# Modulation vectors by VectorE, GpSimd and ScalarE in four feed-forwards instead of by TensorE

## The chip, the cores and the metric

The kernel runs on one core of a Trainium2 chip. The metric is the device time of one execution in microseconds (us), the median of a few runs. A core has five engines with queues of their own, each in order: PE (TensorE, matmuls; PEld is its weight load), DVE (VectorE), ACT (ScalarE), POOL (GpSimd) and SP (SyncE, which issues the transfers here). They meet through semaphores. SBUF is the on-chip memory, PSUM the memory that PE writes.

## The reference, cut to what matters

Two networks of two layers run one after the other on 256 tokens of 1024 features, in float32. The second one is steered by modulation vectors, which come from two conditioning vectors and from nothing else:

```
for i in range(DEPTH):                      # DEPTH = 2
    m_lat = (silu(c) @ ada_w[i] + ada_b[i])      # [9 * 1024]
    m_ctx = (silu(c_ctx) @ ada_w[i] + ada_b[i])  # the same matrix
    sh1, sc1, gt1, sh2, sc2, gt2, sh3, sc3, gt3 = split(m_lat, 9)
    ...
    x = x + 0.5 * gt1 * swiglu(rmsnorm(x, g1) * (1 + sc1) + sh1, wi, wo)
    ...                                     # the context stream alike, with m_ctx
```

So for each layer a matrix of 1024 x 9216 (36 MB) is multiplied by two vectors. Around it stand eight feed-forwards (1024 to 2 x 2816 and back), a recurrent and attention mixer in each layer of the first block, a convolution module in layer 0 of the second block (for both streams, x and the context), and windowed attention in layer 1.

## The kernel before

Features lie on the partitions, tokens along the free dimension; X holds x in columns 0:256 and the context in 256:512. Every weight tile comes by SP into `wraw` (2 buffers of 1 MB, L275), ScalarE casts it to its high part `whi` (L281), VectorE subtracts that to get the low part `wlo` (L282), and PE makes each product from three matmuls (L294 to L296): high by high, high by low, low by high. Each part of eight 128x128 tiles is one 128x1024 pass; five buffers of each part let about two and a half chunks be ready ahead of PE.

A feed-forward has 22 inner tiles and 8 output tiles. In the first block (`ffn1st`, L408 to L430) an inner tile takes 48 matmuls of 256 columns, then VectorE multiplies the result out of PSUM by the norm (L420), ScalarE takes the silu (L422), VectorE multiplies (L424), and the product is split by ScalarE (L373) and VectorE (L374). An output tile takes 66 matmuls and an add into X (L370), and the following norm's input is made (L393, L370 into `big`) with its squares on GpSimd (`Sq`, L335, L341, L342). The second block's feed-forward (`Feed`) does the same for one stream (L889, L890, L373, L374) or both.

After each inner and output tile a `hook` is called. In the two feed-forwards of layer 0 of the first block it is `hook_ada`; in later ones `hook_bg` runs VectorE's share of the context's convolution in between.

The modulation vectors before: `ada(l, g)` is a generator, four of them with 18 steps each. A step loads 1 MB of `ada_w` into one of the large buffers (`big`, 13 of them), and issues four matmuls with 32 stationary columns, each in its own group of 32 columns of PE and each with 512 moving columns, all into one PSUM bank (L748; the profile has two records for each). After 18 steps ScalarE copies the bank out, 4 small matmuls with the selection `sel` bring the result to feature-major order (L756), and VectorE adds the bias (L759). `filler(n)` runs n steps. Layer 0's 36 steps come from `hook_ada`, layer 1's from the convolution of x (34 of them asked for there) and the feed-forward behind it. `prepare(l)` turns the scales into gains before they are used. The order in which instructions stand on each engine is set by a scheduler from the program's order and its own estimates; `after(newest[0])` holds a load behind the newest weight load on SP, and `after(newest[1])` a matmul behind the newest one.

## Time and profile before

| what | before |
|---|---|
| median of 3 runs | 3207.89 us (3207.72 to 3211.8) |
| the profiled execution: span from first to last instruction | 3207.8 us |
| PE busy | 3138.7 us, 98% |
| DVE busy | 1939.8 us, 60% |
| ACT busy | 1468.9 us, 46% |
| POOL busy | 341.5 us, 11% |
| moved by DMA | 536.02 MB, 167 GB/s on average |
| granted clock of TensorE, mean | 0.985 of full speed |

The page gives no time for the profiled execution but its span; it agrees with the median within 0.1 us. A row with `L282` is about line 282 of the kernel before; `out<-in` names what is written and read. "Busy" of PE is the union of modelled matmuls. In a row of the timeline the first number is the start in us from the span's start, the second the length, and x2 merges neighbours of one kind. A DVE or POOL instruction that stands waiting inside itself is counted as busy.

### The profile page before, as it was taken

What the parts mean: (1) busy time and instruction counts of PE and PEld (TensorE: products, weight loads), DVE (VectorE), ACT (ScalarE), POOL (GpSimd) and SP (SyncE); (2) the same over time, 40 slices, a digit from 0 to 9 for tenths busy, and PEclk for the clock granted to TensorE, in tenths of its full rate; (3) what the DMA queues carried; (4) which work ended last, traced back from release to release, by engine and by line L of the source; (5) the groups of instructions that cost most, each with busy time, mean ns of one, the idle gap of its engine ahead of it and who ended that gap; (6) DMA issues with size and microseconds to landing.
All of it is one profiled execution on the core that took longest, in us unless ns stands there. A gap on an engine that the chain in (4) does not pass through costs nothing.

```text
span 3207.8 us, 55462 instructions
## 1 busy us (share of the span) xinstructions
PE 3138.7 (98%) x23080; PEld 2916.9 (91%) x23080; DVE 1939.8 (60%) x3139; ACT 1468.9 (46%) x2421; POOL 341.5 (11%) x410
## 2 busy tenths in 40 slices
PE   9999999999999999999999999999999999999998
PEld 8899899999999999899999998878888888895898
DVE  6557666556558998668767557954333433356554
ACT  4446654445445446545555446643222322246443
POOL 1010102011010010001011025410002000110101
PEclk9999999999999999999999999989999999999999
DMA  7664346764454554345554554775222223230354
GB/s 284 266 231 164 127 163 238 272 221 167 172 183 171 177 188 166 129 160 188 178 175 159 173 169 168 279 285 188 92 87 97 98 88 110 77 112 34 132 177 139
DMA packets 84252, 536.02 MB, mean 167 GB/s; under 512 B 10016, under 2 KB 13088, under 8 KB 32416
## 3 DMA queue, kind: packets, MB, share of 16 engines
q1 hardware_dynamic: 84000, 532.48, 46.9%
q8 instruction: 180, 2.95, 0.4%
q14 instruction: 72, 0.59, 0.0%
HBM read 531.39 MB, written 1.05 MB: 166 GB/s over the span
## 4 chain that ended last, share of the span: by engine, by line
PE 92%; DVE 3%; ACT 1%; POOL 1%; issue 1%; DMA 1%; POOLq 0%; DVEq 0%; SPq 0%; ACTq 0%
PE psmm L294 28%; PE psmm L295 28%; PE psmm L296 28%; PE psad L748 2%; DVE wlo L282 1%; DVE big L370 1%; PE psad L1133 1%; PE psst L1125 1%; PE psst L350 1%; POOL tmp L342 1%; ACT whi L281 1%; DVE tmp L370 1%; PE psst L296 0%; PE psst L294 0%; PE psst L295 0%
## 5 line engine op out<-in xcount | busy, mean ns | idle before, releaser
L294 PE MATMUL psmm<-big,whi 128*128 128x256 f32 (+1 forms) x6546 | 1955.3, 300 | 14.8 <-ACT big L841 10.9
L295 PE MATMUL psmm<-big,whi 128*128 128x256 f32 (+1 forms) x6546 | 1955.6, 299 | 5.0 <-DVE big L370 5.0
L296 PE MATMUL psmm<-big,wlo 128*128 128x256 f32 (+1 forms) x6546 | 1952.6, 299 | 3.1 <-DVE wlo L282 3.1
L281 ACT CAST whi<-wraw 128x1024 fp32r<-128x1024 f32 (+2 forms) x940 | 904.6, 973 | 1320.4 <-PE psmm L295 941.8
L282 DVE TENSOR_TENSOR wlo<-wraw,whi 128x1024 fp32r<-128x1024 f32 (+2 forms) x940 | 1067.2, 1144 | 689.1 <-ACT whi L281 677.9
L294 PEld LDWEIGHTS psmm<-big,whi 128*128 128x128 f32 x6546 | 1260.6, 193 | 88.4 <-issue 19.8
L295 PEld LDWEIGHTS psmm<-big,whi 128*128 128x128 f32 x6546 | 1262.5, 193 | 46.7 <-issue 7.1
L296 PEld LDWEIGHTS psmm<-big,wlo 128*128 128x128 f32 x6546 | 1261.7, 193 | 44.4 <-issue 5.5
L335 POOL TENSOR_TENSOR tmp<-X 128x256 f32<-128x256 f32 x20 | 15.7, 792 | 1670.5 <-DVE X L370 1620.1
L370 DVE SCALAR_TENSOR_TENSOR big<-U,vec,big 128x256 f32<-128x256 f32 x392 | 188.9, 496 | 4.0 <-ACT big L977 0.5
L890 DVE TENSOR_TENSOR tmp<-tmp,psmm 128x256 f32<-128x256 f32 (+1 forms) x120 | 58.9, 491 | 122.8 <-PE psmm L296 118.7
L373 ACT CAST big<-tmp 128x256 fp32r<-128x256 f32 (+1 forms) x210 | 92.5, 441 | 82.8 <-DVE tmp L424 65.1
L420 DVE TENSOR_TENSOR tmp<-psmm,tmp 128x512 f32<-128x512 f32 x88 | 60.7, 690 | 106.3 <-PE psmm L296 105.5
L296 PE MATMUL psmm<-whi,big 128*128 128x256 f32 x416 | 118.3, 284 | 2.0 <-DVE big L370 2.0
L341 POOL TENSOR_TENSOR tmp<-X 128x256 f32<-128x256 f32 x100 | 83.9, 848 | 329.6 <-DVE X L370 272.5
L294 PE MATMUL psmm<-whi,big 128*128 128x256 f32 x416 | 118.8, 286 | 0.1
L295 PE MATMUL psmm<-wlo,big 128*128 128x256 f32 x416 | 118.1, 284 | 0.0
L374 DVE TENSOR_TENSOR big<-tmp,big 128x256 fp32r<-128x256 f32 (+1 forms) x210 | 97.7, 467 | 20.0 <-ACT big L373 19.4
L342 POOL TENSOR_TENSOR tmp<-tmp,tmp 128x256 f32<-128x256 f32 x100 | 102.6, 1030 | 5.3
L370 DVE SCALAR_TENSOR_TENSOR X<-psmm,mods,X 128x256 f32<-128x256 f32 x96 | 43.5, 480 | 74.7 <-PE psmm L296 72.9
L296 PEld LDWEIGHTS psmm<-whi,big 128*128 128x128 f32 x416 | 79.7, 192 | 2.4 <-DVE big L370 2.2
L295 PEld LDWEIGHTS psmm<-wlo,big 128*128 128x128 f32 x416 | 79.8, 192 | 0.1
(271 smaller groups left out, 2012.1 us busy)
## 6 DMA issues: line engine op xcount, KB each, us to landing
big<-ada SPq DMA_DIRECT2D x72, 1024.0 KB, 9.6
wraw<-fi_c SPq DMA_DIRECT2D x66, 1024.0 KB, 4.9
wraw<-fi_d SPq DMA_DIRECT2D x52, 1024.0 KB, 4.9
wraw<-fi_b SPq DMA_DIRECT2D x44, 1024.0 KB, 4.9
wraw<-fi_a SPq DMA_DIRECT2D x43, 1024.0 KB, 4.9
wraw<-fo_c SPq DMA_DIRECT2D x48, 704.0 KB, 4.0
wraw<-qkv SPq DMA_DIRECT2D x24, 1024.0 KB, 4.9
wraw<-pw SPq DMA_DIRECT2D x24, 1024.0 KB, 4.9
```

The lines of the kernel that those rows point to most:

```text
L281: A.copy(hi[:, :e], raw[:, o : o + e])
L282: V.tensor_sub(lo[:, :e], raw[:, o : o + e], hi[:, :e])
L294: T.matmul(o, wh, xh, start=start, stop=False)
L295: T.matmul(o, wh, xl, start=False, stop=False)
L296: newest[1] = T.matmul(o, wl, xh, start=False, stop=stop).ins
L341: G.tensor_tensor(out=q, in0=src, in1=src, op=ALU.mult)
L342: G.tensor_tensor(out=self.acc, in0=self.acc, in1=q, op=ALU.add)
L370: V.scalar_tensor_tensor(o, a, s, b, op0, op1)
L373: A.copy(hi, src)
L374: V.tensor_sub(lo, src, hi)
L420: V.tensor_tensor(out=v2(t), in0=v2(b), in1=pre.Rb, op=ALU.mult)
L748: T.matmul(p_[32 * q : 32 * q + 32, :], cs[:, 4 * h + q, 16 - 2 * b : 48 - 2 * b], raw[:, q * 512 : (q + 1) * 512], start=b == 0 and h == ...
```

## The change

The product with `ada_w` is turned: the matrix is laid out with output features on the partitions, so that each output is a sum along the free dimension of 1024 products. `Modulation.begin` loads silu's argument, the two conditioning vectors repeated on all partitions (`cs`, 1 MB), and takes the silu on ScalarE. `step` loads 256 outputs of `ada_w` (1 MB: two rows of 1024 for each partition) and works on what earlier steps loaded: VectorE multiplies by the context's vector and sums in the same instruction (its product, `junk`, is dropped), GpSimd multiplies by x's vector in place, and one step later ScalarE sums that by a copy with an accumulated output. `end` adds the bias of a whole layer. The steps of layer 0 stand in the same two feed-forwards as before, two of three inner tiles and the first five output tiles; those of layer 1 are moved forward, from the convolution of x and what follows it into the context's and x's first feed-forwards of the second block. The constants `sel`, `c`, `c_ctx` and the tile `cs` of the old form go; there are 14 large buffers for 13.

```diff
-NBIG = 13
+NBIG = 14
...
-        out[f"ada{l}"] = a["ada_w_2"][l].reshape(2, 4, P, 18, 512).transpose(3, 0, 2, 1, 4).reshape(18, 2, P, 2048)
+        out[f"ada{l}"] = a["ada_w_2"][l].T.reshape(36, 2, P, D).transpose(0, 2, 1, 3)
...
-    def ada(l, g):
-        p_ = ps("ad")
-        for b in range(9):
-            for h in range(2):
-                raw = bigt([P, 2048])
...
-                    nc.sync.dma_start(raw, I[f"ada{l}"][9 * g + b, h])
-                yield
-                with after(newest[1]):
-                    for q in range(4):
-                        T.matmul(p_[32 * q : 32 * q + 32, :], cs[:, 4 * h + q, 16 - 2 * b : 48 - 2 * b], raw[:, q * 512 : (q + 1) * 512], start=b == 0 and h == 0, stop=b == 8 and h == 1, tile_position=(0, 32 * q))
...
+    class Modulation:
+        def __init__(self):
+            self.todo = [(l, g) for l in range(2) for g in range(36)]
+            self.cs = self.here = self.made = None
+
+        def begin(self):
+            self.cs = bigt([P, 2, D])
+            with after(newest[0]):
+                nc.sync.dma_start(self.cs, I["cs"])
+            A.activation(self.cs, self.cs, AF.Silu)
+
+        def step(self, l, more=True):
+            if self.made:
+                raw, o = self.made
+                for i in range(2):
+                    A.activation(raw[:, i], raw[:, i], AF.Copy, accum_out=o[:, i, 0:1])
+                self.made = None
+            if self.here:
+                raw, o = self.made = self.here
+                for i in range(2):
+                    junk = tp.tile([P, D], BF16, tag="junk", name=nm("junk"), bufs=1)
+                    V.scalar_tensor_tensor(junk, raw[:, i], 1.0, self.cs[:, 1], ALU.mult, ALU.mult, accum_out=o[:, i, 1:2])
+                    G.tensor_tensor(out=raw[:, i], in0=raw[:, i], in1=self.cs[:, 0], op=ALU.mult)
+                self.here = None
+            if more and self.todo and self.todo[0][0] == l:
+                g = self.todo.pop(0)[1]
+                raw = bigt([P, 2, D])
+                with after(newest[0]):
+                    nc.sync.dma_start(raw, I[f"ada{l}"][g])
+                self.here = raw, mods[:, l, 2 * g : 2 * g + 2, :]
...
-    def hook_ada(kind, i):
-        if i % 3 < 2 if kind == "in" else i % 2:
-            filler(1, keep=2)
+    def hook_ada(l):
+        def hook(kind, i):
+            if (kind, i) == ("out", KT - 1):
+                return
+            if ada.cs is None:
+                ada.begin()
+            elif kind == "in" and i % 3:
+                ada.step(l)
+            elif kind == "out":
+                ada.step(l, i < KT - 3)
+                if i == KT - 2:
+                    ada.end(l)
+        return hook
...
     def hook_x(kind, i):
         back.run(SLACK[kind])
-        if kind == "out" and i > KT - ADA_X:
-            filler(1)
+        hook_ada(1)(kind, i)
...
-            Feed(0, 0, "fi_c0", "fo_c0").run(H, cur, (1,))
+            Feed(0, 0, "fi_c0", "fo_c0").run(H, cur, (1,), hook_ada(1))
...
-            for _ in range(ADA_F):
-                if left > 0:
-                    filler(1)
-                    left -= 1
-                back.run(BG_X / ADA_F)
+            back.run(BG_X)
...
-    hook = lambda *_: filler(1)
-    ff.outs(a, 0, AHEAD, (0, 1), None, hook)
+    ff.outs(a, 0, AHEAD, (0, 1))
...
-    ff.ins(a, AHEAD, FT, H, (0, 1), hook)
-    filler(99)
+    ff.ins(a, AHEAD, FT, H, (0, 1))
```

`Feed` now calls its hook with the number of the tile just done, and the kernel reserves less room for descriptors that GpSimd would make; no transfer here is issued by GpSimd. In the new file the lines named above have other numbers: L274 and L275 are the cast and the subtraction of the weights, L413, L415, L417, L366 and L367 the steps of an inner tile, L753, L754 and L747 the new passes of VectorE, GpSimd and ScalarE.

How the order moves. First, VectorE in the first feed-forward, before: some three inner tiles, with the number of the buffer behind each name.

```order
L282 TENSOR_TENSOR wlo_935<-wraw_932,whi_934 128x1024
L420 TENSOR_TENSOR tmp_851<-psmm_802,tmp_225 128x512
L282 TENSOR_TENSOR wlo_939<-wraw_932,whi_938 128x1024
L282 TENSOR_TENSOR wlo_1008<-wraw_1005,whi_1007 128x1024
L424 TENSOR_TENSOR tmp_855<-tmp_853,tmp_851 128x256
L374 TENSOR_TENSOR big_231<-tmp_855,big_228 128x256
L420 TENSOR_TENSOR tmp_918<-psmm_869,tmp_225 128x512
L282 TENSOR_TENSOR wlo_1012<-wraw_1005,whi_1011 128x1024
L424 TENSOR_TENSOR tmp_922<-tmp_920,tmp_918 128x256
L282 TENSOR_TENSOR wlo_1075<-wraw_1072,whi_1074 128x1024
L374 TENSOR_TENSOR big_231<-tmp_922,big_228 128x256
```

And the change, at the second of the three clusters of steps among the inner tiles of the same feed-forward (big_284 is the conditioning tile):

```order
L753 SCALAR_TENSOR_TENSOR junk_1009,mods<-big_871,big_284 128x1024
L753 SCALAR_TENSOR_TENSOR junk_1012,mods<-big_871,big_284 128x1024
L413 TENSOR_TENSOR tmp_999<-psmm_950,tmp_219 128x512
L275 TENSOR_TENSOR wlo_1101<-wraw_1094,whi_1100 128x1024
L753 SCALAR_TENSOR_TENSOR junk_1086,mods<-big_1015,big_284 128x1024
L417 TENSOR_TENSOR tmp_1003<-tmp_1001,tmp_999 128x256
L753 SCALAR_TENSOR_TENSOR junk_1089,mods<-big_1015,big_284 128x1024
L367 TENSOR_TENSOR big_225<-tmp_1003,big_222 128x256
L413 TENSOR_TENSOR tmp_1076<-psmm_1027,tmp_219 128x512
L753 SCALAR_TENSOR_TENSOR junk_1230,mods<-big_1092,big_284 128x1024
L417 TENSOR_TENSOR tmp_1080<-tmp_1078,tmp_1076 128x256
L753 SCALAR_TENSOR_TENSOR junk_1233,mods<-big_1092,big_284 128x1024
```

The scheduler has gathered the steps: five stand within five inner tiles here, then three or four tiles have none. In the rows shown, six new passes stand within two and a half tiles.

On GpSimd, in the same feed-forward, there were only the squares at its end; now these stand ahead of them, one row for both halves of a step:

```order
L754 TENSOR_TENSOR big_794<-big_794,big_284 128x1024 x2
L754 TENSOR_TENSOR big_871<-big_871,big_284 128x1024 x2
L754 TENSOR_TENSOR big_1015<-big_1015,big_284 128x1024 x2
L754 TENSOR_TENSOR big_1092<-big_1092,big_284 128x1024 x2
L754 TENSOR_TENSOR big_1236<-big_1236,big_284 128x1024 x2
```

Each writes in place what a VectorE pass L753 reads, so it comes behind that one. And ScalarE at the same place, where the sums stand between the casts of the weights:

```order
L747 ACTIVATE big_871,mods<-big_871 128x1024
L415 ACTIVATE tmp_1078<-tmp_1076 128x256
L747 ACTIVATE big_1015,mods<-big_1015 128x1024
L274 CAST whi_1163<-wraw_1161 128x1024
L274 CAST whi_1167<-wraw_1161 128x1024
L366 CAST big_222<-tmp_1080 128x256
L747 ACTIVATE big_1015,mods<-big_1015 128x1024
L747 ACTIVATE big_1092,mods<-big_1092 128x1024
L274 CAST whi_1240<-wraw_1238 128x1024
L274 CAST whi_1244<-wraw_1238 128x1024
```

A sum L747 waits for GpSimd's pass on the same buffer, and the casts behind it wait with it.

## Rows read from the trace of the kernel before

**Rows 1.** The page, part 1: busy us (share of the span) and instructions of each engine.
```profile
PE 3138.7 (98%) x23080; PEld 2916.9 (91%) x23080; DVE 1939.8 (60%) x3139; ACT 1468.9 (46%) x2421; POOL 341.5 (11%) x410
```
**Rows 2.** The page, part 4: the chain that ended last, by engine and by line.
```profile
PE 92%; DVE 3%; ACT 1%; POOL 1%; issue 1%; DMA 1%; POOLq 0%; DVEq 0%; SPq 0%; ACTq 0%
PE psmm L294 28%; PE psmm L295 28%; PE psmm L296 28%; PE psad L748 2%; DVE wlo L282 1%; DVE big L370 1%; PE psad L1133 1%; PE psst L1125 1%; PE psst L350 1%; POOL tmp L342 1%; ACT whi L281 1%; DVE tmp L370 1%; PE psst L296 0%; PE psst L294 0%; PE psst L295 0%
```
**Rows 3.** Windows: length, busy PE, PEld, DVE, ACT, POOL (x), clock, DMA share, GB/s.
```profile
17.00:231.00 214.00, 212.53 (x1737) 194.65 (x1736) 123.33 (x182) 92.96 (x135) 9.32 (x12) 1.00 0.70 263
505.00:702.00 197.00, 196.95 (x1613) 180.56 (x1614) 114.54 (x156) 87.54 (x129) 16.95 (x23) 1.00 0.69 258
741.00:934.00 193.00, 193.00 (x1611) 193.00 (x1610) 113.14 (x154) 90.73 (x138) 21.01 (x22) 1.00 0.52 180
1713.00:1904.00 191.00, 188.93 (x1555) 188.63 (x1556) 107.86 (x151) 87.33 (x131) 17.10 (x18) 0.98 0.52 179
1934.00:2090.00 156.00, 148.61 (x1189) 133.20 (x1188) 129.51 (x247) 94.72 (x193) 80.41 (x115) 0.96 0.58 223
2090.00:2260.00 170.00, 165.17 (x1051) 134.13 (x1051) 82.80 (x142) 62.39 (x103) 10.38 (x12) 0.95 0.59 223
```
**Rows 4.** L748 in all (groups by form), and one step in PE's timeline.
```profile
L748 PE MATMUL psad<-big,cs 128*32 128x512 f32 x576 | 75.7, 609 | 0.0
...
33.22 0.28 PE L295 MATMUL psmm<-big,whi 128*128 128x256 f32 x1
33.34 0.40 PE L296 MATMUL psmm<-big,wlo 128*128 128x256 f32 x2
33.67 1.07 PE L748 MATMUL psad<-big,cs 128*32 128x512 f32 x8
34.67 0.38 PE L294 MATMUL psmm<-big,whi 128*128 128x256 f32 x1
```
**Rows 5.** Windows, L748 alone, in the convolution of x: PE, PEld, clock, DMA share, GB/s.
```profile
1934.00:2090.00 156.00, 16.25 (x136) 3.61 (x136) 0.96 0.58 223
```
**Rows 6.** ScalarE's groups by form: cast of a weight part, read of a sum.
```profile
L281 ACT CAST whi<-wraw 128x1024 fp32r<-128x1024 f32 x804 | 833.8, 1048 | 1076.8 <-PE psmm L295 698.4 <-issue 133.7 <-PE psmm L296 41.1
...
L1110 ACT ACTIVATION_READ_ACCUMULATOR tmp<-psmm,sm 128x1 f32 x32 | 6.9, 216 | 0.0
```
**Rows 7.** VectorE's groups by form: all, then 741:934 (busy us, mean ns, idle before).
```profile
L420 DVE TENSOR_TENSOR tmp<-psmm,tmp 128x512 f32<-128x512 f32 x88 | 60.7, 690 | 106.3 <-PE psmm L296 105.5 <-ACT tmp L366 0.5
...
L282 DVE TENSOR_TENSOR wlo<-wraw,whi 128x1024 fp32r<-128x1024 f32 x62 | 76.1, 1233 | 64.3 <-ACT whi L281 64.3
...
...
L282 DVE TENSOR_TENSOR wlo<-wraw,whi 128x384 fp32r<-128x384 f32 x14 | 7.8, 558 | 12.9 <-ACT whi L281 12.9
```
**Rows 8.** L342 and L1062: POOL's two-input passes, ns min/median/max.
```profile
L342 POOL TENSOR_TENSOR tmp<-tmp,tmp x100: 722/800/1843, 7.4 to 3182.8; 128x256 f32<-128x256 f32 x100
L1062 POOL TENSOR_TENSOR tmp<-tmp,big x5: 1271/1659/2164, 2873.1 to 2901.7; 128x512 f32<-128x512 f32 x5
```
**Rows 9.** DVE's and POOL's timeline at two places where both are at work.
```profile
1129.96 0.47 DVE L370 SCALAR_TENSOR_TENSOR big<-U,vec,big 128x256 f32<-128x256 f32 x1
1130.36 1.68 DVE L282 TENSOR_TENSOR wlo<-wraw,whi 128x1024 fp32r<-128x1024 f32 x2
1131.97 0.96 DVE L370 SCALAR_TENSOR_TENSOR big<-U,vec,big 128x256 f32<-128x256 f32 x1
...
1130.51 2.13 POOL L995 TENSOR_TENSOR tmp<-tmp,big 128x256 f32<-128x256 f32 x1 [1.55 <-DVE big L370]
...
2871.72 2.36 DVE L282 TENSOR_TENSOR wlo<-wraw,whi 128x1024 fp32r<-128x1024 f32 x2 [2.95 <-ACT whi L281]
2873.99 0.68 DVE L1063 TENSOR_TENSOR tmp<-psst,big 128x512 f32<-128x512 f32 x1
...
2873.07 2.16 POOL L1062 TENSOR_TENSOR tmp<-tmp,big 128x512 f32<-128x512 f32 x1 [22.81 <-PE psst L1061]
```
**Rows 10.** Windows, behind x's feed-forward (columns as in rows 3).
```profile
1904.00:1934.00 30.00, 24.45 (x181) 24.10 (x180) 17.51 (x29) 16.23 (x27) 6.73 (x7) 0.83 0.40 141
```

62 lines of the change are left out of this document (20 added, 42 removed).

## Prediction

> **What bounds the kernel now.** I read the page first: PE is busy 3138.7 of 3207.8 us while DVE is busy 60% and POOL 11% [rows 1]. The chain that ended last says the same: 92% of it is PE, and 2% of the span, some 64 us, is the modulation matmul at L748 [rows 2]. So TensorE sets the time, and the change takes work from it. The question is what stands next to it, so I then read a table of six stretches: the four feed-forwards that receive the new work (17:231 and 505:702 in the first block; 741:934 for the context and 1713:1904 for x in the second), and the two stretches in which layer 1's modulation runs now [rows 3]. The reader is to see in it that PE fills each feed-forward, that DVE is at 56 to 59% there and that POOL does almost nothing.
>
> **What is removed.** 72 steps, each of 8 matmul records. All of L748 is 75.7 us of PE [rows 4]; one step alone shows its price in the timeline: ordinary ones start 0.12 us apart (33.22, then two from 33.34 on), and the next one only at 34.67, so the step takes 34.67 - 33.34 - 0.24 = 1.09 us. Layer 0's 36 steps lie in the first two feed-forwards, layer 1's in the last two stretches of [rows 3], 16.25 us of L748 in the first of these two [rows 5].
>
> **What is added.** Each of the 72 steps now has two VectorE multiply-and-sums of 128x1024 (L753 in the new file), two GpSimd multiplies of 128x1024 in place (L754) and two ScalarE sums (L747). By the four hooks 19, 17, 18 and 18 steps are computed in the four feed-forwards. The 72 transfers of 1 MB stay; four loads of the conditioning tile are added. ScalarE's share: 144 passes near 1.05 us, with a read of the sum at 0.216 us [rows 6], 182 us over four stretches in which ACT is idle for 795 - 358.6 = 436 us [rows 3], so I cost it at nothing; if that cover went, the casts of the weights (L281) would be late next. PE gets nothing new. On SP the loads of the modulation weights stay between those of the other weights; a load now waits until ScalarE has summed what its buffer held, and weight loads queue behind it, but there are 14 buffers for 13, and weights are late there only where VectorE is late already: nothing. The bytes fit too: the context's feed-forward moves 180 GB/s, 18 MB more in 193 us make some 275, and 17:231 has run at 263 with DMA at 0.70 [rows 3]. On POOL the sums of squares for the next norm stand between the new multiplies; the last of these comes some four output tiles before the norm is due, about 30 us, which covers its 4.7: nothing.
>
> VectorE: a two-input pass of 128x1024 is the weight subtraction L282, 1233 ns mean in the context's feed-forward [rows 7]; two in a row take 2.36 at 2871.72 [rows 9]. I take 1.2 us, so 2.4 per step. The sum that this form writes out besides has no VectorE row; the nearest, ScalarE's 0.216 us [rows 6], is the upper bound, zero the lower.
>
> GpSimd: there is no 1024-element row. Two-input passes of 256 elements take 722 ns at least, of 512 elements 1271 ns at least [rows 8]. At 0.55 us for every further 256, 1024 elements take 0.72 + 3 x 0.55 = 2.37 us alone, 4.7 per step. POOL has the time: 72 x 4.7 = 341 us of 795. But it does not run beside VectorE. In [rows 9], at 1130.51, a POOL multiply of 256 elements takes 2.13 us instead of 0.72 because two weight subtractions of DVE come first, and the DVE pass behind it at 1131.97 takes 0.96 instead of the 0.47 at 1129.96. At 2873.07 POOL waits for the second of two L282 (they end at 2874.08) and is done 1.15 us later, at 2875.23; L1063, which reads PSUM for one of its inputs, runs inside that at its usual 0.68. So passes with two SBUF inputs and POOL's passes take turns, whole instruction by whole instruction, while a pass with a PSUM input runs beside POOL. Behind a DVE pass 512 elements hold DVE for 1.15 us (0.12 less than alone), hence 1024 for 2.25.
>
> The longest POOL pass in these rows has 512 elements, so that a longer one keeps DVE out to its end is not shown; both lengths that are shown do, and I take the full 2.25 us. [...]
>
> **The sum.** A step costs VectorE's queue 2.4 + 2 x 2.25 = 6.9 us, 72 steps 497 us. VectorE is idle in the four feed-forwards for 795 - (123.3 + 114.5 + 113.1 + 107.9) = 336 us [rows 3]. What doesn't fit is **497 - 336 = +161 us**: VectorE becomes the bound there, PE waits for the subtracted weights (L282), and layer 0's saving on PE is worth nothing.
>
> Four corrections. POOL may run beside passes with a PSUM input: 44 x 0.69 us (L420 [rows 7]) and 76 of 256 elements at 0.47 (44 L890 and 32 L370 into X, by the L370 at 1129.96 [rows 9]) make 66 us at most; a POOL pass is queued behind whichever DVE pass comes, so I take a third, **-20**. VectorE's idle time can't all be used: in the new order the steps stand in clusters of four or five and the last four output tiles of a feed-forward have none. There PE needs 8 us a tile (66 matmuls of 0.12) and VectorE 4.5 (two L282 of 1.2 and two of 0.56, two L370 of some 0.47 [rows 7, 9]), so 4 x 3.5 = 14 us idle in each; the weights that are ready ahead give a part of the rest back. I take 15 us each, **+60**, between none and 24 each (+96). Layer 1's steps leave the last two stretches: half of the 75.7 us of L748 [rows 4], some 37, and about 3 us of selection matmuls with their waits. In 1934:2090, though, DVE is busy 129.5 of 156 us, and POOL builds diagonals, so of 16 us I count half; **-32**, bounds -21 and -40. The order moves nothing else that anyone waits for.
>
> 3207.8 + 161 - 20 + 60 - 32 = 3376.8; I predict **3375 us**. The sum is against the profiled span of 3207.8; the median of the runs is 3207.89, so no conversion is needed. With every bound at its favourable end (66 of overlap, no lost idle time, -40, VectorE passes at 1.1) this case gives 3208 + 161 - 66 - 40 - 14 = 3249; at the other (0.216 for every sum, POOL at 2.37, 96 lost, -21, no overlap) 3208 + 161 + 31 + 17 + 96 - 21 = 3492.
>
> **Rivals.** First, and on the other side: *POOL's work disappears in idle time*. If the turns cost VectorE only its own 2.4 us a step, 72 x 2.4 = 173 us fit into 336 idle, PE stays the bound and the whole 75.7 us less the 8 us of the convolution go: 3208 - 68 = 3140 us. For it: POOL is idle for over 90% of these stretches, and a DVE that waits for PE can let POOL pass for nothing. Against it: [rows 9], and that 173 + 341 is more than 336; it decides once a step takes less than 336 / 72 = 4.7 us of VectorE's queue. Second: *long POOL passes give way in between*, so that half their time blocks: 2.4 + 2.25 = 4.65 a step, 335 us, exactly the idle time. VectorE and PE are then level, layer 0's saving goes into the clusters' waits, layer 1's stays: 3175 to 3250, say 3215. [...]
>
> [...]
>
> **How the numbers follow.** My case 0.60; first rival 0.13; second 0.12, a third of it each faster than before, within 0.2% and slower; third 0.12; 0.03 for slower in a way I have not seen. A measurement tells about 0.2%, 6 us, from no change. Faster: 0.13 + 0.04 = 0.17; same 0.04; slower 0.60 + 0.04 + 0.12 + 0.03 = 0.79. The range runs from 3190, which takes in my case's favourable end and most of the second rival, to 3475, which takes in half of the third; left out are the first rival and the far ends, 0.2 together.
>
> **What would show it.** In the profile after: the four feed-forwards longer by some 35 to 60 us each, with DVE at over 90% in them; PE idle before L294 to L296, released by the subtraction; L282's mean up from 1.1 to 1.2 us to near 2 there, in pairs with POOL passes that last 2.4 to 4 us; and 1934:2260 shorter by about 30 us. [...]

## The result, and the profile after

The changed kernel takes **3441.43 us** (median of 4 runs, 3438.22 to 3443.46) against 3208.89 us of the kernel before on the same chip: 1.0721 times as long, 95% interval 1.0706 to 1.0736. It is slower by 232.5 us; forecast was 166 more than before, with a range up to 3475. The direction came out, and so did the mechanism, VectorE's queue as the bound because its passes take turns with GpSimd's (its new pass, L753, takes 2236 ns in the mean and 1209 at least). The size did not: by the number alone the result lies in the range of the third rival (3435 to 3500: ScalarE's sums wait for GpSimd in front of the weight casts, and PE's clock is lower where it waits, as in [rows 10]), which is taken up below.

The page of the changed kernel, part 1 and part 4, answers to [rows 1, 2]:

```profile
PE 3128.1 (91%) x22472; PEld 2956.2 (86%) x22472; DVE 2395.0 (70%) x3411; ACT 1617.6 (47%) x2707; POOL 773.1 (22%) x554
...
PE 66%; DVE 18%; issue 6%; DMA 6%; ACT 2%; POOL 1%; SPq 0%; DVEq 0%; ACTq 0%; POOLq 0%
```

The share of PE in the chain falls from 92 to 66%, that of DVE rises from 3 to 18%, those of DMA and of issue from 1 to 6% each. Averages over the span hide the place; the windows show it. These are the same four feed-forwards as in the first four rows of [rows 3], between the same weight loads (length, then busy PE, PEld, DVE, ACT, POOL, the granted clock, DMA's share, GB/s):

```profile
17.00:289.50 272.50, 208.67 (x1594) 204.30 (x1593) 239.09 (x255) 131.44 (x209) 121.60 (x50) 0.88 0.56 211
563.50:817.50 254.00, 192.07 (x1480) 189.28 (x1481) 217.69 (x220) 120.22 (x195) 119.64 (x56) 0.87 0.53 198
855.30:1115.80 260.50, 214.83 (x1644) 210.87 (x1643) 230.73 (x226) 130.23 (x212) 125.30 (x58) 0.91 0.57 210
1894.70:2152.30 257.60, 206.49 (x1577) 202.22 (x1578) 223.79 (x223) 126.22 (x203) 124.70 (x54) 0.91 0.56 210
```

Together they last 1044.6 us where they lasted 795. VectorE was busy 458.9 us in them and is now busy 911.3; ACT, at half, is not the bound. Everything that follows rests on two numbers taken from these rows: VectorE's busy time grew by **452.4 us**, and it is still idle for 1044.6 - 911.3 = **133.3 us**. Outside the four, the stretches from behind x's feed-forward to the end of the joint one became shorter: weight loads behind 1904 us of the kernel before come 248.2 us later than they did, those behind 2496 us 231.3, so 17 us are won there.

What VectorE does can be read from its groups by form in the context's feed-forward (855.3:1115.8; busy us, mean ns | idle before), against [rows 7]:

```profile
L275 DVE TENSOR_TENSOR wlo<-wraw,whi 128x1024 fp32r<-128x1024 f32 x62 | 98.5, 1606 | 23.4 <-ACT whi L274 23.3
L753 DVE SCALAR_TENSOR_TENSOR junk<-big,big 128x1024 bf16<-128x1024 f32 x36 | 78.4, 2177 | 0.3
L275 DVE TENSOR_TENSOR wlo<-wraw,whi 128x384 fp32r<-128x384 f32 x14 | 23.0, 1645 | 0.0
```

L275 is the weight subtraction that was L282. Its long form went from 1233 to 1606 ns; the short one, 384 elements, from 558 to 1645: a pass that needs half a microsecond stands for more than one behind a GpSimd pass. The mean mixes passes that meet nothing with passes that stand for a turn: the median of the 76 is 1222 ns, the longest took 3420.

The taking of turns is seen best in one cluster of steps, in VectorE's timeline of the first feed-forward and then GpSimd's of the same place (start, length, engine):

```profile
35.86 1.22 DVE L753 SCALAR_TENSOR_TENSOR junk<-big,big 128x1024 bf16<-128x1024 f32 x1
...
37.34 3.42 DVE L753 SCALAR_TENSOR_TENSOR junk<-big,big 128x1024 bf16<-128x1024 f32 x1
...
41.03 3.36 DVE L753 SCALAR_TENSOR_TENSOR junk<-big,big 128x1024 bf16<-128x1024 f32 x1
...
48.18 4.50 DVE L275 TENSOR_TENSOR wlo<-wraw,whi 128x1024 fp32r<-128x1024 f32 x2
```

```profile
40.85 2.46 POOL L754 TENSOR_TENSOR big<-big,big 128x1024 f32<-128x1024 f32 x1 [1.17 <-DVE junk L753]
44.48 2.35 POOL L754 TENSOR_TENSOR big<-big,big 128x1024 f32<-128x1024 f32 x1 [1.17 <-DVE junk L753]
48.00 2.47 POOL L754 TENSOR_TENSOR big<-big,big 128x1024 f32<-128x1024 f32 x1 [1.17 <-DVE junk L753]
```

A multiply-and-sum that meets nothing takes 1.22 us; one that comes while GpSimd multiplies takes 3.4, that is its own 1.2 and 2.2 more. GpSimd's pass of 40.85 ends at 43.31, and VectorE's of 41.03 ends at 44.39, 1.1 us after it. The one of 37.34 ends at 40.76, 1.1 us after GpSimd's of 37.23, which ends at 39.69. So here too the turn is a whole instruction, for GpSimd passes of 1024 elements, a length that no row of the kernel before had.

Meanwhile PE stands. Its timeline at the same place (idle time before and its releaser in brackets), then two windows:

```profile
46.44 0.58 PE L287 MATMUL psmm<-big,whi 128*128 128x256 f32 x1 [6.04 <-ACT whi L274]
...
51.60 0.58 PE L289 MATMUL psmm<-big,wlo 128*128 128x256 f32 x1 [4.37 <-DVE wlo L275]
```

```profile
46.40:55.10 8.70, 4.29 (x18) 4.00 (x19) 8.70 (x9) 6.38 (x10) 4.09 (x3) 0.50 0.16 39
55.10:61.00 5.90, 5.90 (x51) 5.90 (x50) 5.90 (x4) 1.22 (x3) 4.63 (x2) 1.00 0.29 122
```

In 46.4:55.1, behind the wait of 6.04 us and with that of 4.37 us inside it, the granted clock is 0.50; in 55.1:61, where PE has work throughout, it is 1.00. Such stretches bring the clock of the four feed-forwards down to 0.87 to 0.91. Over the whole run PE waited 143.3 us in front of L289, nearly all of it for the subtraction, and 99.8 us in front of L287, mostly for the cast (part 5 of the page):

```profile
L289 PE MATMUL psmm<-big,wlo 128*128 128x256 f32 (+1 forms) x6546 | 1979.0, 303 | 143.3 <-DVE wlo L275 143.1
L287 PE MATMUL psmm<-big,whi 128*128 128x256 f32 (+1 forms) x6546 | 1975.8, 303 | 99.8 <-ACT whi L274 80.7
```

### The profile page after: what moved, and what is told of

It reads as the page before. It is cut to its first block, busy times and chain, and to the rows that moved or that the text cites. A ratio compares the mean times of both kernels' runs of the same rounds, so it can differ in the third digit from the quotient of the medians.

```text
span 3440.7 us, 55039 instructions
## 1 busy us (share of the span) xinstructions
PE 3128.1 (91%) x22472; PEld 2956.2 (86%) x22472; DVE 2395.0 (70%) x3411; ACT 1617.6 (47%) x2707; POOL 773.1 (22%) x554
## 4 chain that ended last, share of the span: by engine, by line
PE 66%; DVE 18%; issue 6%; DMA 6%; ACT 2%; POOL 1%; SPq 0%; DVEq 0%; ACTq 0%; POOLq 0%
PE psmm L289 20%; PE psmm L288 20%; PE psmm L287 20%; DVE wlo L275 7%; DVE junk L753 5%; ACT whi L274 1%; DVE big L363 1%; DMA wraw<-fo_c 1%; DMA wraw<-fi_c 1%; DVE big L367 1%; DMA wraw<-fi_a 1%; DMA wraw<-fi_b 1%; PE psad L1139 1%; PE psst L1131 1%; PE psst L343 1%
## 5 line engine op out<-in xcount | busy, mean ns | idle before, releaser
L289 PE MATMUL psmm<-big,wlo 128*128 128x256 f32 (+1 forms) x6546 | 1979.0, 303 | 143.3 <-DVE wlo L275 143.1
L287 PE MATMUL psmm<-big,whi 128*128 128x256 f32 (+1 forms) x6546 | 1975.8, 303 | 99.8 <-ACT whi L274 80.7
L288 PE MATMUL psmm<-big,whi 128*128 128x256 f32 (+1 forms) x6546 | 1975.6, 302 | 6.8 <-DVE big L363 5.6
L275 DVE TENSOR_TENSOR wlo<-wraw,whi 128x1024 fp32r<-128x1024 f32 (+2 forms) x940 | 1189.5, 1280 | 564.4 <-ACT whi L274 549.4
L289 PEld LDWEIGHTS psmm<-big,wlo 128*128 128x128 f32 x6546 | 1284.5, 196 | 189.7 <-DVE wlo L275 154.6
L274 ACT CAST whi<-wraw 128x1024 fp32r<-128x1024 f32 (+2 forms) x940 | 896.1, 972 | 1165.8 <-PE psmm L288 680.8
L287 PEld LDWEIGHTS psmm<-big,whi 128*128 128x128 f32 x6546 | 1285.2, 197 | 140.0 <-ACT whi L274 84.2
L288 PEld LDWEIGHTS psmm<-big,whi 128*128 128x128 f32 x6546 | 1286.1, 197 | 42.9 <-DVE big L363 6.9
L754 POOL TENSOR_TENSOR big<-big,big 128x1024 f32<-128x1024 f32 x144 | 421.4, 2936 | 389.8 <-DVE junk L753 328.4
L753 DVE SCALAR_TENSOR_TENSOR junk<-big,big 128x1024 bf16<-128x1024 f32 x144 | 321.9, 2236 | 1.1
L328 POOL TENSOR_TENSOR tmp<-X 128x256 f32<-128x256 f32 x20 | 17.0, 855 | 1200.5 <-DVE X L363 1156.3
L747 ACT ACTIVATE big<-big 128x1024 f32<-128x1024 f32 x144 | 151.8, 1054 | 95.4 <-POOL big L754 95.0
L366 ACT CAST big<-tmp 128x256 fp32r<-128x256 f32 (+1 forms) x210 | 92.4, 441 | 173.8 <-DVE tmp L417 87.7
L896 DVE TENSOR_TENSOR tmp<-tmp,psmm 128x256 f32<-128x256 f32 (+1 forms) x120 | 58.9, 491 | 127.6 <-PE psmm L289 119.0
L334 POOL TENSOR_TENSOR tmp<-X 128x256 f32<-128x256 f32 x100 | 93.7, 946 | 221.8 <-DVE X L363 212.5
L367 DVE TENSOR_TENSOR big<-tmp,big 128x256 fp32r<-128x256 f32 (+1 forms) x210 | 117.6, 561 | 11.9 <-ACT big L366 11.2
L289 PE MATMUL psmm<-whi,big 128*128 128x256 f32 x416 | 118.7, 286 | 2.0 <-DVE big L363 2.0
L287 PE MATMUL psmm<-whi,big 128*128 128x256 f32 x416 | 119.1, 287 | 0.1
```

The costliest lines, as they stand in the source:

```text
L274: A.copy(hi[:, :e], raw[:, o : o + e])
L275: V.tensor_sub(lo[:, :e], raw[:, o : o + e], hi[:, :e])
L287: T.matmul(o, wh, xh, start=start, stop=False)
L288: T.matmul(o, wh, xl, start=False, stop=False)
L289: newest[1] = T.matmul(o, wl, xh, start=False, stop=stop).ins
L334: G.tensor_tensor(out=q, in0=src, in1=src, op=ALU.mult)
```

## Experiments

Each run stands beside a run of the kernel before on the same chip: 3205.05 us for the first four, 3211.29 for the next four, 3210.99 and 3210.43 (medians of 10 and 17 runs) for the last two pairs. Differences are against these. All but the two VectorE-only versions of the last pairs (7 and 12 executions) are single executions; the 17 of the kernel before spread from 3205.9 to 3218.2 us, so a few us more or less in a single one mean little.

### GpSimd's multiplies left out

```diff
-                    G.tensor_tensor(out=raw[:, i], in0=raw[:, i], in1=self.cs[:, 0], op=ALU.mult)
```

> The changed kernel without GpSimd's products (ScalarE sums the raw matrix rows instead, so x's half of the modulation is not computed). Turns theory: without GpSimd's passes VectorE's own passes go back to 1.2 us and a step costs it 2.6 us, 187 us in all against 336 us idle, so TensorE bounds the four feed-forwards again, each near its old length: 3130 to 3180 us. Rival, VectorE's own new work is what slows: stays above 3380 us. Rival, ScalarE's sums in front of the weight casts slow it: little changes either, above 3380 us.

Measured: **3200.2 us**, 4.9 below the kernel before. GpSimd's 144 passes are worth 232.5 + 4.9 = 237 us, the whole loss. But 3200 also misses the expectation (3130 to 3180): VectorE's own passes fit into its idle time by their sum (177.6 us of L753 into 336) and still eat nearly all that PE saves. In the first feed-forward VectorE is busy 166.7 of 210 us, and PE 199.2 (17:227 of this kernel):

```profile
17.00:227.00 210.00, 199.22 (x1599) 197.33 (x1598) 166.68 (x257) 131.25 (x209) 13.00 (x12) 0.97 0.74 275
```

So idle time of VectorE is not free to use even where 43 us of it are left. That is the first sign of the term that failed.

### VectorE's multiply-and-sums left out

```diff
-                    V.scalar_tensor_tensor(junk, raw[:, i], 1.0, self.cs[:, 1], ALU.mult, ALU.mult, accum_out=o[:, i, 1:2])
+    V.memset(mods, 0.0)   # once
```

> The changed kernel without VectorE's products and sums (the context's half of the modulation is not computed), GpSimd and ScalarE as in the change. Turns theory: GpSimd's 144 turns of 2.25 us alone take 324 us of VectorE's 336 us idle time; with the idle time that can't be used (133 us in the changed kernel) the four feed-forwards stay some 20 to 30 us longer each than TensorE needs: 3240 to 3320 us. Rival, VectorE's own work: falls to 3130 to 3180 us. Rival, GpSimd's turns do not block: 3130 to 3180 us as well.

Measured: **3305.48 us**, +100.4, within the expectation. VectorE has no new work here and still sets the time, through its old passes with two SBUF inputs that GpSimd holds up: over the whole run the subtraction takes 120 us more than before (1277 ns in the mean of all its forms for 1144), L367, which was L374, 60 us more (752 ns for 467).

### ScalarE's sums left out

```diff
-                    A.activation(raw[:, i], raw[:, i], AF.Copy, accum_out=o[:, i, 0:1])
+    V.memset(mods, 0.0)   # once
```

> The changed kernel without ScalarE's sums (x's half of the modulation is not summed), so that no weight cast stands behind a wait for GpSimd. Theory that the excess over the forecast (VectorE idle 133 us in the four feed-forwards instead of 60) is ScalarE's queue, held by sums that wait for GpSimd: falls by 50 to 90 us, to 3350 to 3390 us. Rival, the excess is unevenness of the steps (they stand in clusters): 3420 to 3441 us, VectorE's idle time there stays above 110 us. Rival, the sums are the main cause: below 3250 us.

Measured: **3437.67 us**, +232.6: as slow as with them, the case of the expectation's first rival. Sums that wait for GpSimd in front of weight casts, the first half of the third rival, cost nothing here.

### Both sums on VectorE, no GpSimd, no ScalarE

```diff
-                    V.scalar_tensor_tensor(junk, raw[:, i], 1.0, self.cs[:, 1], ...)
-                    G.tensor_tensor(out=raw[:, i], in0=raw[:, i], in1=self.cs[:, 0], op=ALU.mult)
-                    A.activation(raw[:, i], raw[:, i], AF.Copy, accum_out=o[:, i, 0:1])
+                    for q in (1, 0):
+                        V.scalar_tensor_tensor(junk, raw[:, i], 1.0, self.cs[:, q], ..., accum_out=o[:, i, q : q + 1])
```

> All sums on VectorE (four passes a step, nothing on GpSimd or ScalarE), the same places. Turns theory: a step costs VectorE 4 x 1.28 = 5.1 us instead of the 6.3 us by which its busy time grew, 369 us against 336 us idle: 72 x 1.2 = 85 us less, and the waits of ScalarE for GpSimd (95 us, not all on the path) go as well: 3270 to 3350 us, so better than with GpSimd's help. Rival, GpSimd does take work off VectorE: slower than 3441 us.

Measured: **3228.32 us**, +23.3, some 210 us faster than the change and below the expected 3270 to 3350. Giving VectorE twice as many passes of its own is far cheaper than giving half of them to GpSimd: a pass of 1.21 us replaces a GpSimd pass that keeps VectorE out for 2.2 (3.42 - 1.22).

### What the steps were worth on TensorE

```diff
-    todo = [ada(l, g) for l in range(2) for g in range(2)]
+    todo = [ada(0, g) for g in range(2)]      # first kernel: layer 0 only
+    todo = []                                 # second kernel: none
+    V.memset(mods[:, 1], 0.0)                 # mods in the second
...
-            filler(1, keep=2)                 # in the first kernel nothing
+            filler(1)                         # is kept back for layer 1
```

> The kernel before without the 36 modulation steps of layer 1 (their vectors are zero; layer 0's 36 steps stay on TensorE). It measures by itself the term of the sum that the prediction put at -32 us (bounds -21 to -40). If the term was right: 3165 to 3184 us beside a kernel before of 3205, all of the gain between the first weight load of x's convolution and the end of the joint feed-forward. Rival, after the changed kernel, where the same stretches became only 17 us shorter: 3186 to 3192 us, because TensorE's queue waits there anyway and part of the steps' time lay in those waits.

> The kernel before with no modulation work at all (all vectors zero), on any engine: the most that any way of moving this work can gain. If every one of the 72 steps was on the path: 3205 - 75.7 = 3129 us. If layer 0's 36 are (-39 us) and layer 1's are worth what the changed kernel showed (-17 us): 3145 to 3155 us. More than 3160 us would say that TensorE's steps in the first two feed-forwards were partly hidden too.

Measured: **3199.24 us** without layer 1's steps, -12.1, near the rival's case (13 to 19 us below 3205), and **3154.13 us** without any, -57.2, within its expectation. By the weight loads behind x's feed-forward layer 1's steps are worth 14 us in the first kernel and 18 in the second. So they are worth 12 to 18 us, not 32, and the change could have won 57 at the very most; by the weight loads of the second kernel 41 of these are won ahead of the context's feed-forward, where layer 0's steps were. Of this ceiling VectorE's passes alone gave back some 52 (-57.2 to -4.9). Where the 37 us of layer 1's matmuls went is seen in 2090:2180. First the kernel before, all of it and L748 alone:

```profile
2090.00:2180.00 90.00, 85.17 (x626) 69.04 (x626) 50.34 (x94) 41.73 (x78) 10.38 (x12) 0.91 0.72 282
...
2090.00:2180.00 90.00, 16.85 (x120) 2.41 (x120) 0.00 (x0) 0.57 (x1) 0.91 0.72 282
```

then the same stretch without layer 1's steps, where most weight loads come within 5 us of the same times:

```profile
2090.00:2180.00 90.00, 77.55 (x559) 76.00 (x559) 54.78 (x94) 44.44 (x82) 13.77 (x13) 0.85 0.33 113
```

PE had 16.85 us of them there. Without them it is idle 12.4 us of the 90 instead of 4.8, and its clock falls from 0.91 to 0.85: 7.6 us, nearly half of the steps, had filled waits.

### One operand from PSUM

```diff
+            self.cp = pad.tile([P, 1024], F32, tag="ad", name=nm("psad"))
+            for q in range(2):
+                A.copy(self.cp[:, q * 512 : (q + 1) * 512], self.cs[:, 1, q * 512 : (q + 1) * 512])
...
-   V.scalar_tensor_tensor(junk, raw[:, i], 1.0, self.cs[:, 1], ...)
+   V.scalar_tensor_tensor(junk, raw[:, i], 1.0, self.cp, ...)
```

> The change with one thing altered: the conditioning vector that VectorE's multiply-and-sum reads is copied to a PSUM bank once in each feed-forward, so that those passes read one operand from SBUF and one from PSUM (one PSUM buffer of the small transposes is given up for it). If two SBUF operands are what makes VectorE's passes take turns with GpSimd's, these 144 passes fall from a mean of 2.24 us to about 1.3 us and run beside GpSimd's multiplies; VectorE saves up to 135 us of busy time and the whole comes to 3290 to 3350 us. The weight subtraction (two SBUF operands as before) still waits, with a mean near 1.5 us. Rival, the turns go by the engine and not by where the operands lie: the passes stay above 2 us and the whole at 3425 to 3445 us. A second way to miss: the passes get shorter but VectorE's subtractions then meet the same GpSimd multiplies alone, and the whole falls by less than half of the busy time saved (3380 to 3410 us).

Measured: **3329.45 us**, +118.2 where the change has +232.5, within the expectation. VectorE's and GpSimd's timelines of this kernel show why:

```profile
34.64 1.22 DVE L758 SCALAR_TENSOR_TENSOR junk<-big,psad 128x1024 bf16<-128x1024 f32 x1
...
36.12 1.22 DVE L758 SCALAR_TENSOR_TENSOR junk<-big,psad 128x1024 bf16<-128x1024 f32 x1
...
37.26 1.49 DVE L369 TENSOR_TENSOR big<-tmp,big 128x256 fp32r<-128x256 f32 x1
...
43.49 4.51 DVE L275 TENSOR_TENSOR wlo<-wraw,whi 128x1024 fp32r<-128x1024 f32 x2
```

```profile
35.95 9.84 POOL L759 TENSOR_TENSOR big<-big,big 128x1024 f32<-128x1024 f32 x4 [14.57 <-DVE junk L758]
```

Four GpSimd passes run back to back (9.84 us, 2.46 each) while VectorE's multiply-and-sums go by at 1.22 us inside them. A pass with two SBUF inputs there, even one of 256 elements (L369, 0.42 us elsewhere in this timeline), waits. Over the whole run:

```profile
L758 DVE SCALAR_TENSOR_TENSOR junk<-big,psad 128x1024 bf16<-128x1024 f32 x144 | 174.6, 1212 | 2.0 <-DMA big<-ada 0.8
L275 DVE TENSOR_TENSOR wlo<-wraw,whi 128x1024 fp32r<-128x1024 f32 x804 | 1086.5, 1361 | 470.9 <-ACT whi L274 458.2 <-PE psmm L288 2.8 <-PE psst L359 2.1
```

1212 ns for 2236: it is where the operands lie that decides, not the engine. The subtraction, with two SBUF operands as before, keeps its 1361 ns (1354 in the changed kernel). What is left, 118 us, is near the 100.4 of the kernel without VectorE's multiply-and-sums, where the old passes alone take turns.

### Why VectorE is idle 133 us: bunches of steps, and weights that come late

In the changed kernel's first feed-forward, stretches that are VectorE's alternate with stretches that are PE's. Windows of the changed kernel (busy PE, PEld, DVE, ACT, POOL, clock):

```profile
35.00:80.00 45.00, 29.56 (x205) 28.51 (x204) 45.00 (x42) 22.44 (x36) 23.37 (x10) 0.81 0.52 196
80.00:110.00 30.00, 30.00 (x252) 30.00 (x252) 25.78 (x28) 13.99 (x23) 8.92 (x3) 1.00 0.71 277
110.00:155.00 45.00, 30.60 (x215) 29.29 (x215) 42.99 (x43) 24.54 (x40) 22.26 (x8) 0.85 0.37 143
155.00:170.00 15.00, 15.00 (x128) 15.00 (x127) 12.36 (x16) 7.96 (x11) 2.41 (x1) 1.00 0.94 370
170.00:200.00 30.00, 15.00 (x106) 14.50 (x105) 29.88 (x27) 11.94 (x23) 18.65 (x7) 0.72 0.25 98
200.00:215.00 15.00, 15.00 (x128) 15.00 (x127) 8.70 (x13) 7.92 (x13) 0.61 (x1) 1.00 0.69 225
```

Where GpSimd has 7 to 10 passes, DVE is full and PE waits; where it has one to three, PE is full at 1.00 and DVE waits. What is lost in a stretch of the first kind is not won back in one of the second. Nowhere do both stand: laid over each other, the gaps of VectorE and of PE in the four feed-forwards coincide for only 0.5 of VectorE's 133.3 us. So VectorE is idle while PE lives on weights that are ready.

Why it does not run further ahead in that time is told by what ended the waits (who waited, for what: us in total, times, longest), first in the context's feed-forward before (741:934), then in that of the changed kernel (855.3:1115.8):

```profile
DVE wlo L282 <- ACT whi L281: 77.3, 63, 4.2
ACT whi L281 <- PE psmm L295: 73.1, 47, 3.3
...
ACT whi L281 <- DMA wraw<-fi_c: 5.0, 4, 1.8
ACT whi L281 <- DMA wraw<-fo_c: 4.2, 5, 1.0
```

```profile
ACT whi L274 <- DMA wraw<-fo_c: 28.9, 10, 3.9
...
DVE wlo L275 <- ACT whi L274: 23.3, 13, 4.2
...
ACT whi L274 <- DMA wraw<-fi_c: 10.7, 7, 4.1
...
ACT whi L274 <- PE psmm L288: 6.3, 4, 3.3
```

Before, VectorE waited for casts that waited for PE to free one of the five buffers. Now the casts wait for weights that are still on their way. Over the four feed-forwards 104.4 of VectorE's 133.3 us stand in front of the subtraction, and the casts waited 148.7 us for weight transfers (62.2 before) and 27.9 for PE (255.3 before). The loads in turn wait longest for the subtraction, which frees one of the two `wraw` buffers (131.2 us of SyncE's waits in 855.3:1115.8). So a VectorE that was held up gets its next weights late, and has nothing to subtract when it is free. A version with more `wraw` buffers was not tried.

Two kernels tried to take the bunches apart. The first ties the next tile's first VectorE pass behind the newest step, and weight loads behind the newest load of modulation weights:

```diff
-            V.tensor_tensor(out=v2(t), in0=v2(b), in1=pre.Rb, op=ALU.mult)
+            with behind(newest[2]):      # the newest L753
+                V.tensor_tensor(out=v2(t), in0=v2(b), in1=pre.Rb, op=ALU.mult)
...
-                newest[0] = nc.sync.dma_start(raw[:, :E], src).ins
+                with behind(newest[3]):  # the newest load of ada
+                    newest[0] = nc.sync.dma_start(raw[:, :E], src).ins
```

> The change with the same work, but steps tied one to a tile: the weight loads of a tile stand behind the newest load of modulation weights in SyncE's queue, and the first VectorE pass of the next tile behind the newest multiply-and-sum, so no tile has the passes of more than one step piled up behind it. It tests the term that failed: VectorE was idle 133 us in the four feed-forwards of the changed kernel, where the prediction allowed 60. If those gaps come from steps that stand in bunches, some tiles with four passes and some with none, idle time falls to 60 to 90 us and the whole to 3370 to 3405 us. Rival, the gaps are the chain of weight load, ScalarE's cast, VectorE's subtraction that is late after every held-up pass however the steps are spread: idle stays above 115 us and the whole at 3420 to 3450 us.

Measured: **3450.07 us**, +238.8, idle time 158 us (1059.3 - 901.4 over its four feed-forwards): the expectation failed, and its rival's idle time came. The kernel did not do what it was made for. A tie that holds a step ahead of the next tile does not stop it from moving forward, and two steps still stood in one tile; tiles of the first feed-forward took from 3.0 to 22.0 us by the starts of their first VectorE pass. The second kernel cuts a step in two and holds each half behind its own tile's first pass as well as ahead of the next one's:

```diff
-                for i in range(2):
-                    V.scalar_tensor_tensor(junk, raw[:, i], ...)
-                    G.tensor_tensor(out=raw[:, i], ...)
+                with after(newest[4]):   # the first VectorE pass of this tile
+                    newest[2] = V.scalar_tensor_tensor(junk, raw[:, i], ...).ins
+                G.tensor_tensor(out=raw[:, i], ...)
...
-            elif kind == "in" and i % 3:
-                ada.step(l)
+            elif kind == "in":
+                for _ in range(1 if i % 5 else 2):
+                    ada.step(l)          # a half
```

> The change with the same passes, but each step cut in two and the halves spread evenly: one multiply-and-sum and one GpSimd multiply per inner tile of a feed-forward (two at every fifth) and two per output tile, each VectorE pass held behind the first VectorE pass of its own tile and ahead of the next tile's. In the changed kernel a tile of the first feed-forward takes from 3.8 to 18.7 us where TensorE alone needs 5.8: tiles with two steps' passes are VectorE's, tiles with none are TensorE's, and VectorE is idle there. If that is what left 133 us of VectorE's time unused, each tile now needs 3.8 + 3.15 = 7 us of VectorE, idle time falls to 60 to 80 us and the whole to 3360 to 3395 us. Rival: VectorE's gaps come with every pass that waits for GpSimd, because ScalarE's casts and TensorE's buffers fall out of step, however even the passes are: idle above 110 us, the whole at 3415 to 3450 us.

Measured: **3414.29 us**, +203.3: 29 us better than the change, but at the edge of the rival's numbers. The context's feed-forward in three parts, first of the changed kernel, then with halves:

```profile
855.30:930.00 74.70, 64.88 (x518) 63.86 (x516) 65.15 (x77) 41.46 (x68) 32.72 (x19) 0.95 0.56 212
930.00:1095.00 165.00, 131.48 (x977) 128.97 (x978) 151.28 (x138) 79.20 (x130) 82.68 (x34) 0.89 0.57 215
1095.00:1115.80 20.80, 18.48 (x152) 18.04 (x151) 14.30 (x13) 9.57 (x15) 9.90 (x7) 1.00 0.52 170
```

```profile
843.00:918.00 75.00, 68.61 (x551) 67.80 (x550) 55.25 (x74) 40.12 (x64) 22.26 (x16) 0.95 0.59 225
918.00:1083.00 165.00, 131.07 (x990) 128.04 (x989) 162.70 (x145) 83.92 (x140) 104.57 (x38) 0.90 0.58 212
1083.00:1095.50 12.50, 12.50 (x99) 12.50 (x98) 6.53 (x9) 5.35 (x8) 4.12 (x5) 0.92 0.74 231
```

In the middle the idle time went with the bunches: 13.7 us of 165 became 2.3, although 31 of GpSimd's multiplies stand there instead of 27. The two ends are another matter. The end, with two of the multiplies before and none now, was idle 6.5 us and is 6.0. At the start, with five instead of eight, idle time grew from 9.6 to 19.8 us, nearly as much as was won in the middle. VectorE's waits at the start tell where (of the changed kernel, then with halves):

```profile
DVE tmp L896 <- ACT tmp L895: 0.8, 1, 0.8
```

```profile
DVE tmp L906 <- ACT tmp L904: 9.2, 3, 4.6
```

L906 is the first VectorE pass of a tile, the one to which the halves are tied (L896 in the changed kernel). VectorE now stands in front of it until ScalarE has the tile's silu: 8.4 of the 10.2 us come from there. Over all four feed-forwards 115 us stayed idle (1019.7 - 904.5): the waits in front of the subtraction fell from 104.4 to 66.0 us, those in front of a tile's first pass rose from 13.0 to 36.9. So even steps take idle time away, and the ties that make them even add some; how much evenness alone would give was not tried.

### A version for VectorE alone, spread

The runs point away from GpSimd and toward even passes. The next kernel has the halves, both sums on VectorE, and layer 1's steps in three places, the last of them the inner tiles of the joint feed-forward:

```diff
+    def hook_d(kind, i):
+        if ada.cs is None:
+            ada.begin()
+        for _ in range(2):
+            ada.step(1)
...
-    ff.ins(a, AHEAD, FT, H, (0, 1))
+    ff.ins(a, AHEAD, FT, H, (0, 1), hook_d)
+    ada.end(1)
```

> Halves as above, with no GpSimd multiply and no ScalarE sum: VectorE makes both sums of a half (two passes of 1.21 + 0.08 us, 4 a step), and layer 1's steps are spread over three places, 10 or 11 in each of the two feed-forwards of the context and of x and the rest in the inner tiles of the joint feed-forward, where VectorE is busy under half of the time. With bunched passes and two places for layer 1 this came to 23 us more than the kernel before. A tile of layer 0's feed-forwards needs 3.8 + 2.6 = 6.4 us of VectorE beside 6.5 of TensorE before (5.8 without its modulation steps): about even there (-10 to +10 us over both); layer 1's steps cost 0 to +8 us and give back the 12 us that they were worth on TensorE. The whole at 3185 to 3215 us beside 3208. Rival, the passes cost the same wherever they stand: 3220 to 3235 us.

Measured: **3219.23 us** (7 runs), 1.0032 times the kernel before, interval 1.0021 to 1.0044: between the two expectations, next to the rival's. Its trace suggests two things to mend. The conditioning vectors are loaded at the start of each stretch, and in the first a tile behind that load takes 11.8 us where its neighbours take 5.5 and 7.0; two later tiles with four passes each take as long without it, 12.8 and 11.5. And the feed-forwards of the context and of x lose 7 and 6 us, while the joint one with its 14 steps loses none: weight loads are 18 us late ahead of it and 11 behind it. So the vectors were loaded once, and more steps moved there:

```diff
-NBIG = 14
+NBIG = 13
+    csv = cp.tile([P, 2, D], F32, tag="csv", name="csv")
...
-            self.cs = bigt([P, 2, D])
+            self.cs = csv
+            if loaded:
+                return
...
-    ff.ins(a, 0, AHEAD, H, (0,))
-    ff.outs(a, 0, AHEAD, (0, 1))
+    ff.ins(a, 0, AHEAD, H, (0,), hook_d1)
+    ff.outs(a, 0, AHEAD, (0, 1), None, hook_d1)
```

> The VectorE-only version once more, with two things altered. The conditioning vectors (1024 KB to all partitions, and ScalarE's pass over them) are loaded once for the whole program into a buffer of their own in place of one of the 14 big ones; the version before this loaded them at the start of each of five stretches, and there a weight load landed late and one tile took 11.8 us instead of some 6. And of layer 1's 36 steps 8 each stay in the feed-forwards of the context and of x and 20 go to the joint feed-forward, where the version before spent 14 at no cost. If those reloads were the cost of 7 to 9 us in each later feed-forward, three or four of them go (-5 us each): 3219 - 20 = 3190 to 3206 us, beside a kernel before of some 3209: faster than both kernels by a little. Rival, the passes themselves are what costs, in the feed-forwards as in the joint one: 3212 to 3225 us.

Measured: **3206.16 us** (12 runs), at the upper edge of the expectation, 0.9988 times the kernel before, interval 0.9980 to 0.9997. It is the fastest version that computes everything, about 4 us below the kernel before and 235 below the change; with the edge of the interval at 0.9997 the first of these is small. By the weight loads it loses 3 and 6 us in the first two feed-forwards, nothing in the next two, and wins 15 behind them. The two edits of this run were not told apart. In the change itself the single load was tried alone:

> The change as it is, with the conditioning vectors loaded once for the whole program into a buffer of their own (13 big buffers instead of 14). The prediction put the added loads at nothing. If the reloads delayed weight loads at the start of three feed-forwards by some 5 us each, the whole falls from 3441 to 3420 to 3432 us. Rival, in the changed kernel VectorE is the bound there and the late weight loads are hidden behind it: 3436 to 3448 us.

Measured: **3439.39 us**, +229.0: the rival's case. So in the changed kernel the reloads cost nothing that a single run can show, and the prediction's "nothing" for them was right. Whether it would hold for a better version is open, since the single load was not told apart there.

## Why the prediction was right, and where its size was off

The sum of the prediction, term by term, with what the rows of the changed kernel give:

| term | forecast, us | measured, us |
|---|---|---|
| the steps in VectorE's queue, less overlap (497 - 20) | 477 | 452.4 |
| VectorE's idle time before | -336 | -336.1 |
| idle time that could not be used | +60 | +133.3 |
| layer 1's steps gone from the later stretches | -32 | -17 |
| sum | +169 | +232.6 |

The measured column adds up by its making: its first three rows are the lengths of the four feed-forwards taken apart, so its closing proves nothing about causes. Part of the nearness is luck: the first term was 25 us too large and hid as much of the 88 us by which the last two terms were short; without it the same sum ends at 3466 us, near the end of the range.

- **The turns: right.** 452.4 us over 72 steps are 6.28 us a step; forecast were 6.9 less the overlap, 6.6. GpSimd's pass alone was extrapolated from 256 and 512 elements to 2.37 us and its fastest is 2.347. The turns are taken by whole instructions, also at 1024 elements (VectorE's pass of 41.03 ends 1.1 us after GpSimd's of 40.85), which rules out the second rival; and they hang on two SBUF inputs, as the L1063 row of [rows 9] suggested and the PSUM run shows (1212 ns for 2236).
- **"VectorE becomes the bound, layer 0's saving is worth nothing": right.** 143 us of waits for the subtraction stand in front of PE's L289, and the first two feed-forwards are 116 us longer although 41 us of PE's time are gone.
- **"VectorE's idle time can't all be used ... +60, between none and 24 each": the step that failed**, by 73 us. It counted the four output tiles at the end of a feed-forward. The end is the smallest part: 6.5 of the context's 29.8 us. The middle, where steps stand in bunches of four and five, has 13.7 and the start 9.6. The prediction named the bunches, but then summed VectorE's work over a whole feed-forward, as if weights prepared in an idle stretch could feed PE in a full one. The windows above show that they do not, and the waits show that a VectorE that is free mostly waits for a cast whose weights are late. The prediction had put late weight loads at nothing, "late there only where VectorE is late already". How the 73 us divide between the bunches and the late weights is not settled: even halves took 18 us of idle time away, with ties that add waits of their own.
- **Layer 1's -32: off by 14 to 20 us.** By itself it is worth 12 to 18. The convolution's share had been halved for PE's waits there; the same should have been done behind it, in 2090:2180, where PE stands idle in the place of nearly half of the steps.
- **ScalarE's sums and the loads of the conditioning vectors at nothing: right**, by the runs without the sums (+232.6) and with a single load (+229.0). For the weight loads it is not borne out, as said above.
- **The rivals.** "POOL's work disappears in idle time" is excluded. The third rival's range holds the measured 3441, and two signs of it are there: the granted clock is 0.88 and 0.87 in two of the four feed-forwards, and VectorE waits 104.4 us for ScalarE's casts, though that is less than the 223 before. But the queue that it named is excluded: without the sums the kernel is as slow, and the casts wait for weights. As for the clock, by the trace's records it stands at 0.50 for 225 us of the four feed-forwards, behind PE's wait of 6.04 us among others, and VectorE is idle in only 3.9 of these: PE is slow almost only where VectorE sets the time. A run that holds the clock up was not tried; that it costs nothing anywhere is argued, not shown. The range's upper end, 3475, took in half of this rival; no run shows its terms, a cost of the queue in each step and a lower clock that adds to the time: without the sums the kernel is as slow (+232.6), and only 3.9 us of the low clock lie where VectorE is idle.
- **What would show it.** The feed-forwards are 57 to 68 us longer (35 to 60 were named), VectorE is busy 86 to 89% in them (over 90), the subtraction's mean is 1.6 us (near 2), and 17 us are won behind them (30). GpSimd's passes last 2.35 to 3.45 us, as named.

One expectation behind the prediction was off in the same way: VectorE's passes without GpSimd were forecast at 3130 to 3180 us and came to 3200. The same idle time was again taken as usable.

## What to carry to other kernels

Before work goes to GpSimd, look at the operands of what VectorE does in that stretch: here those with two SBUF inputs took turns with GpSimd's, whole instruction by whole instruction (3.4 us for 1.22 beside a GpSimd pass of 2.46), so 144 passes of an engine beside the path cost 237 us on it; with one operand in PSUM a VectorE pass stayed at 1.21 us. Fill idle time tile by tile and not stretch by stretch: here VectorE, busy 56 to 59%, gave back some 52 of 57 us for some 44 us of its own passes in each feed-forward (177.6 / 4). Ask too what the idle engine can do ahead: in the changed kernel most of VectorE's idle time stood before weights that were not there yet, with two buffers to load them into; that more buffers would help was not tested. And first measure what the removed work is worth by leaving it out: layer 1's 37 us of matmuls were worth 12 to 18.

## What the runs showed of the hardware that was not expected

- Reading the sum of a VectorE multiply-and-sum costs 73 to 86 ns (144 of them in the changed kernel); the prediction had bounded it by ScalarE's 216.
- The multiply-and-sum of two float32 inputs takes as long with both in SBUF (1.209 us at least in the changed kernel) as with one in PSUM (1.204 us at least).
- GpSimd's pass is slowed by the turns too: 2347 ns at least, 3282 in the median, and 2553 in the median when VectorE reads one operand from PSUM.
